# Taking the engine barrier out of a kernel's opening block

## The chip, the cores and the metric

The kernel runs on one core of one Trainium2 chip. The metric is the device time of one execution in microseconds, lower is better. A kernel is run several times; medians with lowest and highest are given.

The profile's "span" is the time from the first to the last instruction of the program. The device time is a little longer: in the nine profiled executions of this study the difference lies between 1.34 and 1.37 us, a difference of at most 0.03 us, to which number 4 comes back. The "packet records" named below are the trace's own list of DMA packets (start, length and size of each).

## The reference

```python
def reference(x):                      # x: (32, 512, 1024) float32
    relu_x = np.maximum(x, 0)
    return np.sum(relu_x, axis=-1).astype(np.float32)   # (32, 512)
```

Each of 16,384 rows of 1024 numbers is clamped at zero and summed. 67.1 MB are read, 0.07 MB written.

## The kernel before

The kernel is already tuned. SyncE issues all loads on one queue into three buffers of 64 KB per partition. ScalarE clamps a buffer, VectorE sums its rows, and the next load into that buffer waits until VectorE is through. Towards the end the loads become small and both engines take single rows, so that little is left when the last bytes land (2.6 us of span, from 157.0 to 159.6, in the profile of before).

```python
def issue_ahead_of_the_barrier(tc, n_loads):
    SP = mybir.EngineType.SP
    blocks = tc.nc.main_func.blocks
    opening = blocks[0].instructions
    body = next(b for b in blocks if b.name == tc.start_bb_name).instructions
    loads = [i for i in body if i.engine == SP][:n_loads]
    for i in loads:
        assert isinstance(i, mybir.InstDMACopy)
        body.remove(i)
    at = next(n for n, i in enumerate(opening) if i.engine == SP)
    opening[at:at] = loads
```

The loads that matter here, in the body (cut):

```python
    for j in range(NB):                       # NB = 7 loads of 16 rows, NBUF = 3
        buf = bufs[j % NBUF]
        loaded = load(buf[:, :, :], rows(m, ROWS), j >= NBUF and freed[j - NBUF])
        ...                                   # clamp on ScalarE, sum on VectorE
```

So the first three loads wait for nothing, and from the fourth on each waits for VectorE.

## Time and profile before

| | before |
|---|---|
| device time, first three runs | 161.21 us (161.05 to 161.30) |
| span of the profiled run | 159.6 us |
| DMA queue, share of 16 engines | 98.1% |
| busiest compute engine (VectorE) | 74% |
| first load issued / landed / first ACTIVATE | 0.00 / 21.7 / 21.73 us |
| second load issued / landed | 0.79 / 41.0 us |
| ScalarE's table load | 0.79 to 2.07 us |

How to read it: a load is *issued* when SyncE hands it to the queue and has *landed* at the last of the sixteen updates that the trace has of its semaphore (the first load's at 21.71 us). ACTIVATE is the instruction with which ScalarE clamps; the table load (1.28 us) is the one counted instruction that the trace has on ScalarE ahead of the first ACTIVATE. `SPq` and `PEq` are the instruction sequencers of SyncE and TensorE. The DMA queue, at 98.1%, is the bound; the prediction reads the opening step by step. The question is whether anything that the barrier delays is needed at once.

One more view of before carries the argument: what SyncE's queue waited for (who, for whom, us in total, times, longest).

```profile
SPq L97 <- DVE res L123: 122.9, 5, 51.3
SPq L107 <- ACT io L130: 28.2, 2, 27.3
...
SPq L260 <- PEq L260: 0.2, 1, 0.2
```

The last line is the barrier as SyncE saw it: a wait of 0.2 us. (The view guesses TensorE's sequencer as the releaser; in the trace, GpSimd's second semaphore instruction at 0.67 us raises the semaphore on which the four others wait.) The first line is 122.9 us of waiting for VectorE to free buffers. Even that does not starve the queue, because the load before is still under way at each such issue: the fourth load is issued at 52.87 us, and the third lands 7.5 us later.

### The profile page before, as it was taken

The numbers are of one execution on the slowest core, as the hardware profiler recorded it, in microseconds if no ns is written. First come the engines' busy times: TensorE is split into PE (matmuls) and PEld (weight loads), VectorE is DVE, ScalarE is ACT, GpSimd is POOL, SyncE is SP. The second block draws the span as 40 slices with busy tenths as digits, with TensorE's granted clock in tenths as the row PEclk, the third lists the DMA queues.
The fourth block names the chain that finished last, engine by engine and source line by source line (L and its number), as shares of the span: only waits on it lengthen the run. The fifth ranks groups of instructions, "written<-read, shape, count | busy, mean of one in ns | idle before, by whom it ended". The sixth has DMA issues, their size and how long they took to land.

```text
span 159.6 us, 129 instructions
## 1 busy us (share of the span) xinstructions
DVE 117.5 (74%) x41; ACT 104.2 (65%) x50; POOL 0.2 (0%) x4
## 2 busy tenths in 40 slices
DVE  0000000009999499994999999999999999999986
ACT  3000059990799708996099941999339992499985
POOL 0000000000000000000000000000000000000000
DMA  7996996996996998979969969969969969798994
GB/s 263 525 525 263 525 526 263 525 525 263 526 493 296 525 411 378 525 328 460 526 279 509 525 263 526 525 263 525 525 263 525 509 279 525 337 452 386 412 405 127
DMA packets 2304, 67.18 MB, mean 421 GB/s; under 512 B 640, under 2 KB 896, under 8 KB 1024
## 3 DMA queue, kind: packets, MB, share of 16 engines
q1 hardware_dynamic: 2304, 67.18, 98.1%
HBM read 67.11 MB, written 0.07 MB: 421 GB/s over the span
## 4 chain that ended last, share of the span: by engine, by line
DMA 43%; DVE 34%; ACT 17%; another core or an unknown queue 3%; SPq 0%; issue 0%; DVEq 0%
DMA io<-in_x_dram 43%; DVE res L123 32%; ACT io L115 17%; DVE io L140 1%; SPq L97 0%; DVE piece L219 0%; DVE piece L140 0%; DVEq L218 0%
## 5 line engine op out<-in xcount | busy, mean ns | idle before, releaser
L123 DVE TENSOR_REDUCE res<-io 128x8 f32<-128x8192 f32 (+2 forms) x9 | 101.1, 11286 | 39.9 <-ACT io L115 39.9
L115 ACT ACTIVATE io<-io 128x8192 f32<-128x8192 f32 (+2 forms) x9 | 81.7, 9111 | 46.9 <-DMA io<-in_x_dram 46.9
L130 ACT ACTIVATE io<-io 128x1024 f32<-128x1024 f32 x20 | 20.9, 1045 | 5.9 <-DMA io<-in_x_dram 5.7
L140 DVE TENSOR_SCALAR_CACHE_REDUCE io<-io 128x1024 f32<-128x1024 f32 (+1 forms) x14 | 15.5, 1165 | 0.7 <-DMA io<-in_x_dram 0.6
L130 ACT ACTIVATION_READ_ACCUMULATOR io<-io 128x1 f32 x20 | 3.8, 188 | 0.0
L115 ACT ACT_TABLE_LOAD x1 | 1.3, 1283 | 0.8 <-PEq L260 0.8
L140 DVE DVE_READ_ACCUMULATOR io<-io 128x1 f32 x14 | 1.2, 82 | 0.0
L219 DVE TENSOR_SCALAR_CACHE_REDUCE piece<-piece 128x406 f32<-128x406 f32 x1 | 0.6, 576 | 0.1
L140 DVE TENSOR_SCALAR_CACHE_REDUCE piece<-piece 128x260 f32<-128x260 f32 x1 | 0.4, 424 | 0.0
L260 POOL MEMSET const-bfloat16-1.0<- 128x1 bf16 x1 | 0.1, 102 | 0.0
L260 POOL MEMSET const-uint8-127<- 128x1 uint8 x1 | 0.1, 102 | 0.0
L260 POOL MEMSET const-float32-0.0<- 128x1 f32 x1 | 0.1, 99 | 0.2 <-issue 0.2
L260 POOL MEMSET const-float32-1.0<- 128x1 f32 x1 | 0.1, 99 | 0.0
L140 DVE DVE_READ_ACCUMULATOR piece<-piece 128x1 f32 x1 | 0.1, 83 | 0.0
L219 DVE DVE_READ_ACCUMULATOR piece<-piece 128x1 f32 x1 | 0.1, 82 | 0.0
## 6 DMA issues: line engine op xcount, KB each, us to landing
io<-in_x_dram SPq DMA_DIRECT2D x1, 4096.0 KB, 21.6
io<-in_x_dram SPq DMA_DIRECT2D x1, 2048.0 KB, 26.1
io<-in_x_dram SPq DMA_DIRECT2D x1, 1204.0 KB, 28.6
io<-in_x_dram SPq DMA_DIRECT2D x1, 512.0 KB, 29.4
piece<-in_x_dram SPq DMA_DIRECT2D x1, 202.0 KB, 29.3
piece<-in_x_dram SPq DMA_DIRECT2D x1, 130.0 KB, 29.3
io<-in_x_dram SPq DMA_DIRECT2D x7, 26.9
out_dram<-res SPq DMA_DIRECT2D x1, 55.0 KB, 1.6
```

What stands on the lines that cost most here:

```text
L115: i = nc.scalar.activation(out=ap, in_=ap, func=RELU)
L123: nc.vector.tensor_reduce(out=res[:, m : m + n], in_=ap, axis=mybir.AxisListType.X, op=ADD).wait_op(sems.act, n_act, "sem-ge").then_inc(se ...
L130: i = nc.scalar.activation(out=ap, in_=ap, func=RELU, accum_out=res[:, m : m + 1])
L140: i = nc.vector.tensor_scalar(out=ap, in0=ap, scalar1=0.0, scalar2=None, op0=MAX, op1=ADD, accum_out=accum_out,)
L219: nc.vector.tensor_scalar(out=last[:, :], in0=last[:, :], scalar1=0.0, scalar2=None, op0=MAX, op1=ADD, accum_out=res[:, NT - 2 : NT - 1],) ...
L260: nc = _bacc.Bacc("TRN2", target_bir_lowering=False, num_devices=1)
```

## The change

The intent: no engine reads the constants that GpSimd writes, and each engine waits on its own semaphores for the data it uses; so the barrier guards nothing, and it can go. (This is read from the code. In the traces of before no instruction but GpSimd's four MEMSETs names a constant.) The constants are still written. The first load stays the first instruction of SyncE.

```diff
-    issue_ahead_of_the_barrier(tc, EARLY)
+    open_without_barrier(tc, EARLY)
 ...
-def issue_ahead_of_the_barrier(tc: tile.TileContext, n_loads: int):
+def open_without_barrier(tc: tile.TileContext, n_loads: int):
 ...
     body = next(b for b in blocks if b.name == tc.start_bb_name).instructions
+    for i in list(opening):
+        if isinstance(i, (mybir.InstDrain, mybir.InstEventSemaphore)):
+            opening.remove(i)
     loads = [i for i in body if i.engine == SP][:n_loads]
```

## The prediction

> **What bounds the kernel now.** I read the engine shares first, then the DMA queue part, then stretches of 20 us, then the chain in order of time, and last the opening microsecond.

> ```profile
> span 159.6 us, 129 instructions
> DVE 117.5 (74%) x41; ACT 104.2 (65%) x50; POOL 0.2 (0%) x4
> q1 hardware_dynamic: 2304, 67.18, 98.1%
> ```

> No compute engine is over 74%, but the packets of the one DMA queue fill 98.1% of what 16 engines could do in the span. The kernel has to read 32 x 512 x 1024 x 4 bytes = 67.1 MB. The stretches say whether that stream ever stops (columns: stretch, its length, busy time of DVE, ACT and POOL with instruction counts, clock, DMA share, GB/s):

> ```profile
> 0.00:1.00 1.00, 0.00 (x0) 0.21 (x1) 0.20 (x4) 1.00 0.00 0
> 1.00:21.00 20.00, 0.00 (x0) 1.07 (x1) 0.00 (x0) 1.00 1.01 423
> 21.00:41.00 20.00, 5.38 (x1) 13.86 (x1) 0.00 (x0) 1.00 1.08 469
> 41.00:61.00 20.00, 17.89 (x2) 14.45 (x2) 0.00 (x0) 1.00 0.97 419
> ...
> 121.00:141.00 20.00, 20.00 (x4) 14.97 (x13) 0.00 (x0) 1.00 0.96 416
> 141.00:157.00 16.00, 15.35 (x28) 15.16 (x30) 0.00 (x0) 1.00 0.95 398
> ```

> Nothing moves in the first microsecond; afterwards the share stays at 0.95 or more up to 157 us. In the packet records the first load packet starts at 1.01 us, the last load packet ends at 157.4 us, and there is no moment between them at which no packet is in flight: 67.1 MB / 156.4 us = 429 GB/s. So the time is: 1.0 us before the stream, 156.4 us of stream, and about 2.2 us of last sum and last store. Only what starts the stream earlier, fills a hole in it, or shortens the end can move the time.

> The opening shows where the barrier stands (columns: start, length, what):

> ```profile
> 0.00 1.60 SPq L97 DMA_DIRECT2D io<-in_x_dram  x3
> 0.23 0.10 POOL L260 MEMSET const-float32-0.0<- 128x1 f32 x1 [0.23 <-issue]
> ...
> 0.79 1.28 ACT L115 ACT_TABLE_LOAD   x1 [0.79 <-PEq L260]
> 21.73 13.86 ACT L115 ACTIVATE io<-io 128x16384 f32<-128x16384 f32 x1 [19.66 <-DMA io<-in_x_dram]
> ```

> The first load is issued at 0.00, before the barrier[...]. The three issues are one row here; asked by shorter windows they stand at 0.00 to 0.38, 0.79 to 1.12 and 1.17 to 1.60. The barrier therefore lies between the first load and the second. ScalarE's table load is the only counted instruction that the barrier holds (0.79 us)[...].

> [...]the first packet at 1.01 us is 0.63 us after the end of the first issue at 0.38. [...]the second load is issued at 0.79 but lands 40.2 us later, 19.3 us after the first one, because it stands behind it. [...]I take the cost of the barrier from the start of what follows it, not from the 8 to 181 ns of its own records.

> **The change, part by part.** By the instruction order, eleven sequencer instructions go: a drain and a semaphore wait on each of ScalarE, TensorE, VectorE and SyncE, and a drain and two semaphore instructions on GpSimd. Nothing is added, no counted operation moves, and every load, sum and store keeps its order and its own waits.
> 1. First load: already ahead of the barrier. 0.00 us.
> 2. Second and third loads: SyncE needs only its branch after the first issue. In the trace the second issue comes 0.07 us after the barrier's last SyncE instruction, so I estimate it at 0.38 + 0.07 = 0.45 instead of 0.79: 0.34 us earlier. Both descriptors then wait in the ring behind the first load, which lands at 21.7 us. The third load has still more: it begins to move only about when the second lands, at 41.0 us. Of the 0.34 us, 0.00 reaches the stream.
> 3. ScalarE's table load: from 0.79 to about 0.15, where its own drain stands now, thus 0.64 us earlier. It ended at 2.07 and was not wanted until 21.73: 19.66 us of slack, so 0.00.
> 4. VectorE first works at 35.6 us, TensorE never, and GpSimd's four constants are not read. 0.00.
> 5. The later loads wait for VectorE to free a buffer, and that begins with the first landing, which doesn't move. They also have slack: the fourth load is issued at 52.87 us, while the third lands only at 60.4, so 7.5 us of queued work is left.
> 6. The end (last piece, sum, store) has the same instructions. 0.00.
> Sum: 0.00 us on the path, out of some 0.4 us that the barrier takes from SyncE. The measured time (161.21) is 1.6 us longer than the profiled span; I take that remainder as unchanged.

> **The rivals.** *The chain's head is worth what it shows.* The chain that ended last, in order of time, begins so:

> ```profile
> 0.72 0.07 issue
> 0.79 40.24 DMA io<-in_x_dram
> 41.04 0.02 issue
> 41.06 13.86 ACT io L115
> ```

> Read literally, the end hangs on the second load's issue, which the barrier delayed; then 0.34 us would come off: 160.9. Against it: 40.24 us is no transfer time for 8.4 MB, which takes 19.3; over half of it is waiting behind the first load, so an earlier issue lengthens this piece by as much. I give it one chance in ten.
> *The three issues collide at the start.* Without the pause, the second and third issues come at about 0.45 and 0.83, before the first packet at 1.01. If feeding more descriptors delayed the first load's packets, the stream would start later, by an estimated 0.1 to 0.4 us (an issue's 0.33 to 0.42 us at most): up to 161.6. Against it: already before, the second issue (0.79 to 1.12) runs across the first packets without a visible hole. One in ten.
> *The start of the measured time hangs on the barrier.* If the clock outside the span began or ended with an engine that the barrier held, up to the barrier's 0.7 us might come off: 160.5. The profile doesn't show the outside; but each engine's first record lies at 0 to 0.31 us in any case, before the barrier. One in twenty.
> *Something reads a constant too early.* This would show as a wrong result and not in time[...].

> **Range and chances.** The three runs of before span 161.05 to 161.30, thus 0.25 us of noise. My middle is the median, 161.2 us. Noise of 0.15 each way plus the first two rivals, each worth some 0.3 us, give 160.9 to 161.5. Two per cent is 3.2 us, over four times all the barrier's 0.7 us; so within 2% has 0.985, faster 0.01 and slower 0.005, these two left for a disturbance that nothing in the profile hints at.

> **What would show each step right or wrong.** In the changed profile: the span 159.6 give or take 0.2; the three issues as one row of about 1.25 us from 0.00 instead of 1.60; the table load at about 0.15; the first ACTIVATE still at 21.7, the second at 41.1, the third at 60.4; the chain's second-load piece longer than 40.24 by what its start is earlier; DMA share still 0 in the first microsecond. I am wrong if the first ACTIVATE moves by over 0.2 us either way (then the start of the stream depends on what the other engines or SyncE do), or if it stays and the time yet changes (then the difference is outside the span or at the end).

That no engine reads GpSimd's constants rests on the code and on the names in the trace (see The change). That the second load stands behind the first is in the packet records of before: when the first load has landed, at 21.71 us, 128 packets of 64 KB (8.4 MB, its own size) and 16 of 4 bytes have ended, and no others. That the stream itself could not run faster, which "only what starts the stream earlier, fills a hole in it, or shortens the end" takes for granted, was the author's estimate and is not shown.

## The result, and the profile after

| | runs | median | lowest to highest |
|---|---|---|---|
| before | 6 | 161.19 us | 161.05 to 161.30 |
| after | 6 | 161.07 us | 161.02 to 161.19 |

The result is correct, and the ratio of the times is 0.9995 with a 95% interval of 0.9982 to 1.0008: the same.

The changed kernel's page has these lines for the span, the engines and the queue:

```profile
span 159.7 us, 118 instructions
...
DVE 117.5 (74%) x41; ACT 104.2 (65%) x50; POOL 0.2 (0%) x4
...
q1 hardware_dynamic: 2304, 67.18, 98.0%
```

The reader is to see that eleven instructions are gone (129 before) and that the engines' busy times are those of before. The opening, in order of time (start, length, what):

```profile
0.00 1.33 SPq L97 DMA_DIRECT2D io<-in_x_dram  x3
0.12 1.28 ACT L115 ACT_TABLE_LOAD   x1
...
21.78 13.86 ACT L115 ACTIVATE io<-io 128x16384 f32<-128x16384 f32 x1 [20.38 <-DMA io<-in_x_dram]
```

The three issues end at 1.33 instead of 1.60 us. The table load starts at 0.12 instead of 0.79. And the first ACTIVATE starts at 21.78, where it was 21.73: the 0.67 us that ScalarE gained has become waiting for the first load (19.66 us before, 20.38 us now).

The chain that ended last begins so in the changed kernel (start, length, what):

```profile
0.00 0.38 SPq L97
0.38 0.05 issue
0.43 40.65 DMA io<-in_x_dram
41.09 0.02 issue
41.11 13.86 ACT io L115
```

Add start and length of the DMA piece: 0.43 + 40.65 = 41.08 now, 0.79 + 40.24 = 41.03 before. The piece began 0.36 us earlier and ended where it did. The stretches show the same stream (columns as in the prediction):

```profile
0.00:1.00 1.00, 0.00 (x0) 0.88 (x1) 0.20 (x4) 1.00 0.00 0
1.00:21.00 20.00, 0.00 (x0) 0.40 (x1) 0.00 (x0) 1.00 1.01 423
21.00:41.00 20.00, 5.33 (x1) 13.86 (x1) 0.00 (x0) 1.00 1.08 469
```

Again no packet starts in the first microsecond, and then come 423 and 469 GB/s as before. (The view counts a packet whole in the stretch in which it starts, so a share can pass 1.00; the mean over the stream is the one to read.) What changed is ScalarE's column: the table load's 1.28 us now lies mostly in the first row. VectorE's 5.33 instead of 5.38 us is the first landing, 0.05 us later.

### The profile page after: what moved, and what is told of

The parts are those of the page before. It is cut to its first block, busy times and chain, and to the rows that moved or that the text cites. A ratio compares the mean times of both kernels' runs of the same rounds, so it can differ in the third digit from the quotient of the medians. Undisturbed runs are those within 1.5% of the kernel's fastest.

```text
span 159.7 us, 118 instructions
## 1 busy us (share of the span) xinstructions
DVE 117.5 (74%) x41; ACT 104.2 (65%) x50; POOL 0.2 (0%) x4
## 2 busy tenths in 40 slices
DMA packets 2305, 67.18 MB, mean 421 GB/s; under 512 B 641, under 2 KB 897, under 8 KB 1025
## 3 DMA queue, kind: packets, MB, share of 16 engines
q1 hardware_dynamic: 2304, 67.18, 98.0%
## 4 chain that ended last, share of the span: by engine, by line
DMA 43%; DVE 34%; ACT 17%; another core or an unknown queue 3%; SPq 1%; issue 0%; DVEq 0%
DMA io<-in_x_dram 43%; DVE res L123 32%; ACT io L115 17%; DVE io L140 1%; SPq L97 1%; DVE piece L219 0%; DVE piece L140 0%; DVEq L218 0%
## 5 line engine op out<-in xcount | busy, mean ns | idle before, releaser
L115 ACT ACTIVATE io<-io 128x8192 f32<-128x8192 f32 (+2 forms) x9 | 81.7, 9110 | 47.6 <-DMA io<-in_x_dram 47.6
```

The lines of the kernel that those rows point to most:

```text
L115: i = nc.scalar.activation(out=ap, in_=ap, func=RELU)
```

## The experiments

My theory: the time is set by when the first load's data starts to flow; all else that the barrier held has some 20 us of slack. The rivals: the second load's issue is on the path, as the chain shows it (chain head); ScalarE's start is on the path; two effects cancel, an earlier queue against colliding issues; and the start of the measured time hangs on the barrier. Seven more runs were made, two of them repeats of a kernel, each beside the kernel before on the same chip. All gave correct results.

### 1. The barrier kept, the first load put back behind it (barrier_first)

In the kernel before:

```diff
-EARLY = 1
+EARLY = 0
```

> The kernel before with the barrier kept and the first load put back behind it, in its place in the body. The theory (only what starts the first load's data counts): the barrier's last SyncE record now comes ahead of the first issue; without an issue of its own to wait for, the barrier closes on GpSimd's drain, so I work out an issue at about 0.70 us where it stood at 0.00, and the whole stream later by that: time 161.8 to 161.9 us, first ACTIVATE 21.7 us after the first issue, as ever. The chain-head rival (the second load's issue counts): the second issue moves from 0.79 to about 1.1, so 161.5. A rival that a barrier at the opening costs nothing wherever it stands: 161.2.

Measured: 161.91 us (161.89 to 162.06, 5 runs) against 161.29 us for before (161.17 to 161.46, 9 runs); ratio 1.0041, interval 1.0028 to 1.0054. So 0.6 to 0.7 us longer. The opening of this kernel, in order of time:

```profile
0.72 1.28 ACT L115 ACT_TABLE_LOAD   x1 [0.72 <-PEq L260]
0.73 1.32 SPq L97 DMA_DIRECT2D io<-in_x_dram  x3
22.64 13.86 ACT L115 ACTIVATE io<-io 128x16384 f32<-128x16384 f32 x1 [20.63 <-DMA io<-in_x_dram]
```

The first issue is at 0.73 us, close to the 0.70 expected (in before GpSimd's drain ends at 0.48 and SyncE's, behind its issue, at 0.56; the table load, 0.79 there, starts 0.07 earlier here), and the first ACTIVATE follows 21.9 us after it. The barrier does cost something when the first load stands behind it. The second issue moved only from 0.79 to 1.15, which the chain head would have put at 0.36 us; the interval, 0.45 to 0.87 us, leaves that out and holds the first issue's 0.73.

### 2. No barrier, and the first load not moved (no_barrier_not_early)

In the changed kernel:

```diff
-EARLY = 1
+EARLY = 0
```

> The changed kernel (no barrier) with the first load left in its place in the body, behind SyncE's branch. Theory: with no barrier to pass, only a branch of some 0.07 us stands ahead of the first issue, so the time is that of the changed kernel within 0.1 us, 161.1 to 161.2, and 0.6 to 0.7 us under the kernel with the barrier first. That would mean that the move of the load and the removal of the barrier buy the same thing, and that the second of them buys nothing. If the removal had a worth of its own that the changed kernel hid (two effects that cancel), this kernel would differ from the changed one by over 0.1 us.

Measured: 161.19 us (161.12 to 161.37, 5 runs), ratio to before 0.9993, interval 0.9979 to 1.0006. The changed kernel in the same rounds (number 4) had 161.18. So without a barrier the early move buys 0.01 us or nothing, while without the move the barrier's removal buys 161.91 - 161.19 = 0.72 us, and with the barrier the move buys 161.91 - 161.29 = 0.62 us. The two are two ways to the same gain, and the kernel before had already taken it by the move. This answers where the worth of the barrier went: not off the chip, but into an earlier change.

### 3. The barrier kept, three loads ahead of it (three_early)

In the kernel before:

```diff
-EARLY = 1
+EARLY = 3
```

> The kernel before with all three unblocked loads ahead of the barrier: three issues back to back as in the changed kernel, but ScalarE held at the barrier until SyncE comes to it, at about 1.6 us. Theory: same as before, 161.1 to 161.2; the table load moves from 0.79 to about 1.6 and stays hidden. Rival of cancelling effects (earlier queueing gains 0.3 us, colliding issues lose it): here and in the changed kernel the first packet would come later than 1.01 us after the first issue, or the first ACTIVATE earlier than 21.7. Rival that ScalarE's start counts: 0.8 us longer, 162.0.

Measured: 161.25 us (161.21 to 161.37, 5 runs), ratio 0.9999, interval 0.9987 to 1.0012. Its opening:

```profile
0.00 1.32 SPq L97 DMA_DIRECT2D io<-in_x_dram  x3
...
1.72 1.28 ACT L115 ACT_TABLE_LOAD   x1 [1.72 <-PEq L260]
21.94 13.86 ACT L115 ACTIVATE io<-io 128x16384 f32<-128x16384 f32 x1 [18.93 <-DMA io<-in_x_dram]
```

ScalarE starts 0.93 us later than before and the time is the same, so its start is not on the path. The three issues back to back are those of the changed kernel; the first packet still comes 1.00 us after the first issue in the packet records (1.01 before), so no start was lost to a collision. The first ACTIVATE at 21.94 is within what the kernel before shows itself (21.73 and, in number 7, 21.98).

### 4. The changed kernel again (after_again)

No edit but a comment.

> The changed kernel once more, to see whether the 0.1 us between the medians (161.07 against 161.19) is real. Theory: it is noise, or at most what lies outside the profiled span; the ratio's interval holds 1.000 and the medians lie within 0.15 us. Rival (the start of the measured time hangs on the barrier): the changed kernel faster by 0.1 us or more again, with an interval that leaves out 1.000, while its span is no shorter.

Measured: 161.18 us (161.15 to 161.34, 5 runs) against 161.29; ratio 0.9995, interval 0.9982 to 1.0007. The interval holds 1.000 as the theory expected, but the mean was 0.08 us under that of before for the second time. Whether so little is real could not be told from this; number 7 was made for it. As to the outside of the span: the profiled run has 161.34 us and a span of 159.99, thus 1.35 us, against 160.99 - 159.63 = 1.36 us for before. So the rival's 0.7 us is out. A trace of it is left: in the four profiled executions without a barrier the difference is 1.34 to 1.35 us, in the five with one 1.36 to 1.37. That is 0.02 us, in every one of them, and a quarter of the 0.08; why is not shown.

### 5. A barrier ten times as long (hold_half)

GpSimd clears half of the third load's buffer ahead of its drain, in the kernel before:

```diff
+HOLD = [8]
 ...
+    for n in HOLD:
+        nc.gpsimd.memset(BUFS[2][:, :n, :], 0.0)
+    held = list(body[n_body:])
 ...
+    opening[at:at] = held
```

(`at` is the place of GpSimd's drain, and `BUFS` are the kernel's buffers.)

> The kernel before with its barrier kept but made long: GpSimd clears 8192 elements per partition of the third load's buffer ahead of its drain, so that ScalarE, VectorE and SyncE's second and third loads are held until a time R that I guess at 5 to 15 us instead of 0.7. Theory: the second load's descriptors only have to be in the ring before the first load is through, at about 21 us, and ScalarE's table load (1.3 us) before the first landing at 21.7; so as long as R is under about 19 us the time is that of before, 161.2 to 161.4, with the first ACTIVATE still at 21.7 to 22.1. Chain-head rival: the second issue is on the path, so the time grows by R less 0.7, thus 5 to 14 us. Rival that ScalarE's start counts: as much.

Measured: 161.28 us (161.20 to 161.32, 4 runs) against 161.25 (161.08 to 161.69, 9 runs); ratio 0.9996, interval 0.9977 to 1.0014. The opening, in order of time:

```profile
0.36 6.92 POOL L41 MEMSET io<- 128x8192 f32 x1
7.58 1.28 ACT L130 ACT_TABLE_LOAD   x1 [7.58 <-PEq L275]
22.05 13.86 ACT L130 ACTIVATE io<-io 128x16384 f32<-128x16384 f32 x1 [13.19 <-DMA io<-in_x_dram]
```

And the head of its chain:

```profile
7.52 0.07 issue
7.58 33.76 DMA io<-in_x_dram
41.35 0.02 issue
```

The release is now at 7.5 us, ten times as late as before, for ScalarE, VectorE and SyncE's second and third loads alike. The second load is issued at 7.58 and lands at 41.34: 6.8 us later issued, 0.3 us later landed, in which the first load's landing was late too (first ACTIVATE 22.05). The chain head and ScalarE's start, which would have cost about 6.8 us, are out.

### 6. The second load behind the first one's landing (second_after_first)

In the changed kernel:

```diff
+        if j == 1:
+            nc.sync.wait_ge(sems.loads[0], 16)
         loaded = load(buf[:, :, :], rows(m, ROWS), j >= NBUF and freed[j - NBUF])
```

> The changed kernel with SyncE waiting for the first load's landing before it issues the second: the issue moves from 0.43 to about 21.8 us, past the end of the slack. Theory: the stream now has one hole, from the first load's last packet (21.35 us) to the first packet of the second load, 1.0 us after the issue as at the start, so 21.8 + 1.0 - 21.35 = about 1.4 us, and the time becomes 162.5 to 162.8: 21 us of delay cost 1.4. Chain-head rival: 161.1 + 21.3 = 182. Rival that the ring never lies empty for want of an issue (the queue hides anything): 161.2.

Measured: 163.66 us (163.53 to 163.96, 4 runs) against 161.25; ratio 1.0147, interval 1.0128 to 1.0165: 2.4 us longer. That is the right order, and far from the chain head's 182, but 0.9 us over the top of my 162.5 to 162.8. Its first and second ACTIVATE:

```profile
22.11 13.86 ACT L115 ACTIVATE io<-io 128x16384 f32<-128x16384 f32 x1 [20.71 <-DMA io<-in_x_dram]
...
44.03 13.86 ACT L115 ACTIVATE io<-io 128x16384 f32<-128x16384 f32 x1 [8.06 <-DMA io<-in_x_dram]
```

The second load landed 21.9 us after the first instead of 19.3, so 2.6 us were lost. The packet records part this in two. The hole in which no packet is in flight lasts from 21.74 to 23.07, 1.3 us, which I had expected. But from its first to its last packet the second load then takes 23.07 to 43.66, 20.6 us, where its eight packets on each engine (128 on sixteen), at the 2.42 us of a later packet, make 19.3: another 1.3 us. The sixteen DMA engines do not start together (this load's first packets start between 23.07 and 24.02 us), and most of those first packets of 64 KB take 3.0 to 3.5 us, the later ones 2.42. (In the other runs, where the second load stands behind the first, it takes 19.8 to 20.2 us from first to last packet, but it starts before the last packet of the first has ended: 20.92 and 21.35 us in before.) My estimate had counted the hole and left out this run-up.

### 7. The kernel before against itself (before_again)

No edit but a comment.

> A control: the kernel before, word for word but for a comment, against itself. In two batches the changed kernel's mean was 0.08 us under that of before (0.05%), with intervals that held 1.000. If the order of the runs or their small number makes such a difference, this control shows one as large, 0.05 us or more; if it shows less, the 0.08 us may be the barrier's. Theory: 161.1 to 161.3, ratio within 0.0005 of 1.

Measured: 161.22 us (161.03 to 161.26, 5 runs) against 161.25 (9 runs, two of them at 161.67 and 161.69); ratio 0.9990, interval 0.9976 to 1.0005. The same kernel differs from itself by 0.13 us in the mean of all these runs, more than the 0.08 us by which the changed kernel was under before. My expected 0.0005 was too narrow. So the 0.08 us can't be credited to the barrier; beyond the 0.02 us outside the span (number 4), a real effect of a few hundredths of a microsecond is neither shown nor excluded.

What the scatter is made of can be read from the profiles: span less start of the first ACTIVATE is 159.63 - 21.73 = 137.90 for before, 159.67 - 21.78 = 137.89 for after, and 159.99 - 22.13 = 137.86 for the changed kernel's second profile. The whole difference between these executions, 0.36 us of span, lies ahead of the first landing; everything after it repeats within 0.05 us.

The packet records say where ahead of it. In all nine profiles the first packet starts 1.00 to 1.02 us after the first issue, so the first byte does not move with the scatter. What varies is the run-up: the last of the sixteen DMA engines is through its first packet 4.44 us after the first issue in before, 4.52 in after, 4.72 in before_again and 4.83 in after_again. From there to the first ACTIVATE it is 17.24 to 17.30 us in all nine. So the slowest engine in the first five microseconds makes the difference. With a barrier this run-up is 4.44 to 4.75 us in five profiles, without one 4.52 to 4.88 in four; the two ranges overlap, and no effect of the barrier on it is shown.

## Why the prediction was right

The prediction was 161.2 us within 160.9 to 161.5, "within 2%" at 0.985. Measured: 161.07, then 161.18. By its own steps:

1. *First load, 0.00.* Held: issued at 0.00, first packet at 1.00 us (1.01 before).
2. *Second and third loads, 0.34 us earlier, 0.00 reaches the stream.* The second issue moved from 0.79 to 0.43 (0.45 estimated, with 0.07 us for a branch that has no record of its own in the trace; the gap was 0.05), the DMA piece of the chain grew from 40.24 to 40.65, and its end stayed at 41.0 to 41.1. Shown further by number 5, where 6.8 us of delay cost nothing, and bounded by number 6, where an issue at 22.11 us comes too late; where between 7.58 and 22.11 us the slack ends was not measured. One size was off: I expected the row of three issues to last about 1.25 us and it lasts 1.33, because the issues straight after another took 0.42 to 0.43 us and not 0.33 (0.43 to 0.86 and 0.90 to 1.33 after; 0.79 to 1.12 before).
3. *Table load 0.64 us earlier, hidden.* It starts at 0.12 (0.15 estimated), and ScalarE's wait grew instead. Number 3 moved it 0.93 us later and number 5 6.8 us later, at no cost.
4. and 6. *Other engines and the end, 0.00.* VectorE's 117.5 us is that of before, the queue's share is 98.0% (98.1 before), and span less first ACTIVATE is the same to 0.01 us.
5. *Later loads.* Their issues follow the first landing: the fourth is at 52.87 before and 52.92 after, with its 7.5 us of slack intact.

Of the rivals, the chain's literal head is out by numbers 1, 5 and 6. The collision is out: number 3 and the changed kernel start their first packets as before, and in numbers 5 and 6, where no second issue comes before 7.58 and 22.11 us, the first ACTIVATE is at 22.05 and 22.11, as late as with three issues in a row (21.78 to 22.15). The measured time's start is out as a matter of 0.7 us: what lies outside the span is 0.02 us less without the barrier (number 4). No result shows a constant read early: all are correct.

One of my tests was set too tight. I wrote that I should be wrong if the first ACTIVATE moved by over 0.2 us. In the second profile of the changed kernel it is at 22.13, 0.40 later than in the first profile of before. But the kernel before itself was at 21.98 in its second profile, and a kernel with the long barrier at 22.05. The first landing scatters by some 0.4 us from execution to execution, with the run-up of the engines (number 7), and I had taken one profile for its fixed place. The same scatter made "span 159.6 give or take 0.2" too tight: the second profile has 160.0.

Some of the prediction's figures were off, without weight for the answer. The last load packet ends at 157.0 us, not 157.4, so the stream lasts 156.0 us (430 GB/s) and the end 2.6. The 1.6 us outside the span set a median beside another execution's span; the profiled execution itself took 160.99 us, so it is 1.36. And a noise of 0.15 plus a rival of 0.3 us would have asked for 0.45 us each way, not 0.3. That the range held owes something to the median: the spread of 0.25 us came from three runs, and two of the 29 runs of the unchanged kernel (161.67 and 161.69) lie above 161.5.

What stays open: why the engines' run-up differs from one execution to the next, and whether the barrier moves the time by a few hundredths. The runs are too few for an effect of 0.05%.

## What to carry to other kernels

In this kernel the barrier cost only what the first thing needed behind it waited; once the first load of the stream that bounds the kernel was issued ahead of the barrier, removing the barrier bought nothing measurable more, and of the two measures one was enough (0.62 us for the move, 0.72 for the removal, each alone). Elsewhere, ask first what is needed at once behind the barrier. A chain's DMA piece that was much longer than its bytes need (40.24 us against 19.3) was mostly queueing, and an earlier issue only lengthened it (to 40.65): compare start plus length, not start. Before crediting a tenth of a microsecond to a change, run the unchanged kernel against itself.
